# A two-layer decoder step on one core: weight folding under the recurrence, wide unit tiles in the MLP, one block stored split

## The chip, the cores and the metric

The kernel runs on one core of a Trainium2 chip. The metric is device time in microseconds: the median of three runs before is 2588.51 us (2587.13 to 2591.58). PE is TensorE, DVE is VectorE, ACT is ScalarE, POOL is GpSimd, and SP is SyncE, whose queue issues the DMAs.

## The reference, cut to what matters

1024 prompt tokens and 8 decode tokens go through two layers. Layer A is a gated linear recurrence of six heads beside a cross-attention; layer B is a sliding-window attention over keys and values made from layer A's output, again beside a cross-attention. Each layer has this frame:

```python
hn = rms_norm(h, norm_pre_mix[l])           # layer B: kv = rms_norm(h, kv_norm) @ w_kv as well
proj = hn @ w_in                            # queries, gates, values ...
mix = concat([tok_out, x_out]) @ w_out[l]
h = h + rms_norm(mix, norm_post_mix[l])
u = square(relu(rms_norm(h, norm_pre_mlp[l]) @ w_up[l]))     # 1024 -> 4096
h = h + rms_norm(u @ w_down[l], norm_post_mlp[l])            # 4096 -> 1024
```

## The kernel before, in words

Features lie on the partitions, the N = 1032 tokens on the free axis. An fp32 product is three float32r matmuls of high and low parts (`mm3`, lines 264 to 266), so each operand has to be split: ScalarE copies the high part (line 208), VectorE or GpSimd subtracts it for the low part (`tt`, line 81). `X` holds the split operand that moves through TensorE.

Outside the MLP a weight tile is 128 x 1024. It is loaded into a raw tile (tag `wr`, two buffers), split into a tile with tag `ws` (three buffers), and used for three chunks of 344 tokens (`dense_chunk`), whose sums go to a PSUM bank with tag `dn` (two of them; `ax` has four, `ac` two).

In layer A, `weave` runs the recurrence of one head (`hgrn_head`) beside the dense products of the next head. `out_late` ends the output projection. `post_norm` puts the steps of a norm on a list `bg`, from which `tick` takes them between products.

`fold_w` prepares 20 weight tiles of layer B: it loads one, multiplies 12 of them by a norm's gain on GpSimd, splits it on ScalarE and VectorE and stores both parts to DRAM (`wfd`), from which layer B loads them. Before the change these 20 calls are handed to layer A's `mlp` and run beside its down products, at the units listed in `SIDE`.

`mlp` splits both dimensions in halves and makes seven block products where eight would be plain. Up: four plain tiles, then 14 pairs of tiles with seven products each; the squared results and their sums go to DRAM as blocks "11", "12", "21", "22" and 1 to 4 (`hidden_sums`, `store`). Down: products 1, 7, 5, 6, 3, then 2 and 4, each a list of 16 units (g, m): four 128-row blocks of hidden features by one output tile. For products 1 to 3 a unit covers both chunks of 258 tokens (24 matmuls a chunk pair and g); for 2 and 4 there are separate units for each chunk. `hidden` loads a hidden block, 258 tokens at a time, into a `ct` tile and splits it into `X`; `weight_split` splits the unit's 128 x 512 weights, four units ahead. Norms of the second token half run beside product 2, that of the first half's first chunk beside product 4, the last one after it; layer B's first products (`w0`, two query tiles `cq`, the values in `swa_values`) begin beside that last one.

The code is written in program order, and a scheduler sets the order on each engine from it. In layer A the down stage takes 995.5 to 1416.6 us of the span, in layer B 2223 to 2574.4 us, with the same matmuls.

## Time and profile before

| | us |
|---|---|
| median of 3 runs | 2588.51 |
| profiled execution | 2591.9 |
| its span | 2590.1 |
| layer A: recurrence with the dense products of the next heads (part) | 190 to 560 |
| layer A: output projection and plain up tiles | 560 to 694 |
| layer A: pairs of up tiles | 694 to 995 |
| layer A: down products 1, 7, 5, 6, 3 / product 2 / product 4 | 995.5 to 1277 / to 1350.5 / to 1416.6 |
| layer B: first products | 1416.6 to 1505 |
| layer B: down products 1, 7, 5, 6, 3 / product 2 / product 4 | 2223 to 2464.4 / to 2518 / to 2574.4 |

A stage's row gives the busy time of each engine in it. PEclk is the granted TensorE clock as a share of full speed, a mean of its two levels, 1.2 and 2.4 GHz (0.5 and 1). What a wait or an edit costs is read in its own stage. The two down stages hold the same matmuls, one with folding beside it and one without.

### The profile page before, as it was taken

How to read it: one execution, taken by the hardware profiler on the slowest of the kernel's cores; microseconds unless marked ns; L12 is line 12 of the kernel's file. 1: busy time of each engine (PE TensorE's matmuls, PEld its weight loads, DVE VectorE, ACT ScalarE, POOL GpSimd, SP SyncE). 2: the span in 40 equal slices, each digit the busy share in tenths (PEclk: the TensorE clock that was granted, in tenths of full speed). 3: DMA queues.
4: the chain of work that ended last, by engine and by line, in shares of the span. 5: the costliest groups of instructions: out<-in, count | busy, mean ns of one | idle time of the engine just before them, and what ended most of it. 6: DMA issues, size and time to landing. Idle time of an engine off the chain costs nothing. (4 is left out here: it accounts for less than half of the span.)

```text
span 2590.1 us, 47277 instructions
## 1 busy us (share of the span) xinstructions
PE 2364.5 (91%) x17067; PEld 2282.3 (88%) x17067; DVE 1838.9 (71%) x3200; ACT 1159.1 (45%) x2688; POOL 1362.1 (53%) x1109
## 2 busy tenths in 40 slices
PE   7989999998889999988988799978988999999997
PEld 6889999997889998988978688768988999999996
DVE  7668666746977667898586266774587767787587
ACT  6663433534423333445554255564442333444453
POOL 4545444445755555677555243443576555446655
PEclk9999999998899999989988899989999999999998
DMA  4313222223355448777553133324336444764462
GB/s 163 132 54 100 86 83 75 74 90 115 102 176 149 144 140 273 238 254 274 181 178 109 60 111 107 117 85 150 110 105 173 152 148 136 230 184 136 111 204 85
DMA packets 265446, 362.01 MB, mean 140 GB/s; under 512 B 32938, under 2 KB 200426, under 8 KB 265196
## 3 DMA queue, kind: packets, MB, share of 16 engines
q1 hardware_dynamic: 265212, 358.99, 44.3%
q8 instruction: 134, 2.20, 0.4%
q14 instruction: 100, 0.82, 0.1%
HBM read 242.70 MB, written 112.99 MB: 137 GB/s over the span
## 5 line engine op out<-in xcount | busy, mean ns | idle before, releaser
L264 PE MATMUL dn<-X,ws 128*128 128x344 f32 (+1 forms) x1288 | 426.9, 332 | 31.2 <-DVE X L213 17.4
L265 PE MATMUL dn<-X,ws 128*128 128x344 f32 (+1 forms) x1288 | 420.2, 326 | 0.0
L266 PE MATMUL dn<-X,ws 128*128 128x344 f32 (+1 forms) x1288 | 419.8, 326 | 0.0
L81 DVE TENSOR_TENSOR X<-ct,X 128x258 fp32r<-128x258 f32 (+2 forms) x457 | 313.5, 725 | 92.6 <-ACT X L208 86.3
L81 POOL TENSOR_TENSOR ws<-wr,ws 128x512 fp32r<-128x512 f32 (+1 forms) x118 | 215.1, 1825 | 202.9 <-ACT ws L208 200.3
L264 PEld LDWEIGHTS dn<-X,ws 128*128 128x128 f32 x1288 | 250.1, 194 | 42.8 <-DVE X L213 19.8
L208 ACT CAST X<-ct 128x258 fp32r<-128x258 f32 (+2 forms) x466 | 174.7, 409 | 181.3 <-DMA ct<-u 140.2
L265 PEld LDWEIGHTS dn<-X,ws 128*128 128x128 f32 x1288 | 249.8, 194 | 1.8 <-issue 0.4
L266 PEld LDWEIGHTS dn<-X,ws 128*128 128x128 f32 x1288 | 249.4, 194 | 1.6 <-issue 0.8
L264 PE MATMUL ax<-X 128*128 128x258 f32 x736 | 208.9, 284 | 9.5 <-DVE k L81 9.5
L265 PE MATMUL ax<-X 128*128 128x258 f32 x736 | 208.8, 284 | 0.0
L266 PE MATMUL ax<-X 128*128 128x258 f32 x736 | 208.5, 283 | 0.0
L81 POOL TENSOR_TENSOR p<-p,sm 128x512 f32<-128x512 f32 (+2 forms) x92 | 83.0, 927 | 144.2 <-DVE sm L390 53.4
L208 ACT CAST ws<-wr 128x512 fp32r<-128x512 f32 (+1 forms) x122 | 95.8, 789 | 130.9 <-PE ax L266 45.9
L265 PE MATMUL ac<-X 128*128 128x258 f32 x512 | 149.4, 292 | 0.7 <-POOL X L81 0.7
L264 PEld LDWEIGHTS ax<-X 128*128 128x128 f32 x736 | 140.0, 190 | 10.6 <-DVE k L81 10.6
L266 PE MATMUL ac<-X 128*128 128x258 f32 x512 | 148.7, 290 | 0.0
L264 PE MATMUL ac<-X 128*128 128x258 f32 x512 | 148.2, 290 | 0.0
L265 PEld LDWEIGHTS ax<-X 128*128 128x128 f32 x736 | 139.9, 190 | 0.0
L266 PEld LDWEIGHTS ax<-X 128*128 128x128 f32 x736 | 139.6, 190 | 0.0
L264 PE MATMUL dn<-X 128*128 128x258 f32 x320 | 96.2, 301 | 33.1 <-DVE X L81 29.2
L81 POOL TENSOR_TENSOR X<-p,X 128x512 fp32r<-128x512 f32 (+1 forms) x56 | 82.6, 1487 | 55.1 <-ACT X L208 47.3
(645 smaller groups left out, 8128.3 us busy)
## 6 DMA issues: line engine op xcount, KB each, us to landing
ct<-u SPq DMA_DIRECT2D x480, 129.0 KB, 2.9
u<-k SPq DMA_DIRECT2D x392, 129.0 KB, 2.4
wr<-wu SPq DMA_DIRECT2D x112, 256.0 KB, 3.2
wfd<-ws SPq DMA_DIRECT2D x40, 512.0 KB, 4.1
ws<-wfd SPq DMA_DIRECT2D x26, 512.0 KB, 5.6
wr<-wia SPq DMA_DIRECT2D x25, 512.0 KB, 3.5
p<-hs SPq DMA_DIRECT2D x22, 516.0 KB, 5.3
c<-wd SPq DMA_DIRECT2D x40, 256.0 KB, 4.8
```

Of the source, the lines that this page charges most:

```text
L81: return eng.tensor_tensor(out, a, b, op=op)
L208: A.copy(hi, src)
L264: T.matmul(ps, wh, xl, start=first, stop=False, skip_group_check=more)
L265: T.matmul(ps, wl, xh, start=False, stop=False, skip_group_check=more)
L266: T.matmul(ps, wh, xh, start=False, stop=last, skip_group_check=more)
```

## The change

- The 20 calls of `fold_w` move from layer A's down stage to its recurrence, four to each of the first five heads, and each becomes two steps, load and fold. The raw weight now uses a `wr` tile, the split one a `ws` tile, and one DMA stores both parts.
- In the down stage, products 1, 7, 5, 6 and 3 load and split hidden blocks 516 tokens wide, from six places (`ust`) in two `ws` tiles.
- Block "21" is split where it is made (`split_21`, in the up pairs) and kept in DRAM as high and low parts (`u21`); product 2 loads both straight into `X`. Product 2 becomes one list of 16 units with both chunks (256 and 260 tokens; two tiles' first chunks share a bank), so its weights are split once, not twice.
- Of the weight splits' subtractions, product 2's all go to GpSimd, and of product 4's one in three to VectorE; before, every second one of both.
- `plain_sums` is cut into loads and sums, taken one at a time from the fifth pair on instead of at the second and third.
- `dense_bank`: in the output projection of layer A, in the plain up tiles of both layers and in layer B's first products, sums alternate between `ax` and `dn`.
- The norms of the down stage use `ac` banks, at a rate of 1.6 steps a unit in product 2; the last one sums eight squared rows on TensorE (`direct`) instead of adding them by fours first.
- Layer B's first products: both `cq` tiles of the token chunk that is ready come ahead of what waits for the last norm.

On ScalarE in the recurrence of layer A, between steps of a head. `ws` is a split weight, `wr` its raw tile, `k`, `q`, `t` and `r` tiles of a head. Before:

```order
L594 ACT_TABLE_LOAD
L594 ACTIVATE k_2180<-k_2179 128x344
L595 ACTIVATE k_2179<-k_2179 128x344
L208 CAST r_2272<-p_2175 128x512
L208 CAST ws_2673<-wr_2671 128x1024
```

Now:

```order
L208 CAST ws_2211<-wr_2209 128x1024
L665 ACTIVATE ct_1993<-q_1860 128x344
L705 COPY t_1677<-k_154 128x16x16 x2
L665 ACTIVATE ct_2060<-q_2029 128x344
L705 COPY t_1677<-k_154 128x8x32 x2
L208 CAST ws_2339<-wr_2242 128x1024
L705 COPY t_1677<-k_154 128x4x64 x2
L665 ACTIVATE ct_2104<-q_2029 128x344
L705 COPY t_2204<-k_1681 128x128x2 x2
L208 CAST ws_2375<-wr_2373 128x1024
```

Before, the weight cast ahead of `ws_2673` stands 16 rows further up. Now three casts of weights stand within ten rows: `ws_2211` and `ws_2375` are dense weights, `ws_2339` (raw tile `wr_2242`) is a folded one between them.

On TensorE at the end of layer A's MLP, where `t` and `p` hold the squares of the last norm and `dn_14692` is a product of layer B. Before:

```order
L265 MATMUL dn_14692<-X,p_14687 128x344
L266 MATMUL dn_14692<-X,p_14686 128x344
L160 MATMUL ax_14727<-ones,t_9943 86x1 x3
L180 MATMUL ax_14737<-ct_14735,ones 128x258
L160 MATMUL ax_14946<-ones,p_14722 86x1
L160 MATMUL ax_14946<-ones,p_14724 86x1
```

Now:

```order
L271 MATMUL ax_14428<-ws_14236,X 128x256
L272 MATMUL ax_14428<-ws_14236,X 128x256
L160 MATMUL ac_14283<-ones,t_10242 86x1 x3
L270 MATMUL dn_14300<-X,p_14294 128x344
L270 MATMUL dn_14387<-ws_14233,X 128x256
L271 MATMUL dn_14387<-ws_14233,X 128x256
```

Before, the last norm's two sums (`ax_14727`, then `ax_14946`, over squares of its input and of its output) have only the broadcast `ax_14737` between them, and the values (`dn_14781`) come after. Now the values `ax_14428` stand ahead of the first sum and a `cq` and a values product (`dn_14300`, `dn_14387`) behind it, before the broadcast.

On SP's queue in product 2 of layer A. `X` is the split operand, `u21s` the block stored split, `hs` the layer's output, `wd` weights. Before:

```order
L1307 DMA ct_13343<-u_0_5913 128x258
L1307 DMA ct_13368<-u_0_5913 128x258
L1307 DMA ct_13393<-u_0_5913 128x258
L878 DMA hs_82<-q_9918 128x258
L878 DMA hs_82<-k_9919 128x258
L878 DMA hs_82<-q_9920 128x258
L1307 DMA ct_13418<-u_0_5913 128x258
L878 DMA hs_82<-k_9922 128x258
L878 DMA hs_82<-k_9923 128x258
```

Now:

```order
L1343 DMA X<-u21s_6052 128x2x516 x8
L1296 DMA r_10234<-wd 128x512 x2
L1296 DMA r_10235<-wd 128x512
L1343 DMA X<-u21s_6052 128x2x516
L892 DMA hs_82<-q_10215 128x258
L1343 DMA X<-u21s_6052 128x2x516
L892 DMA hs_82<-k_10216 128x258
L892 DMA hs_82<-q_10217 128x258
L892 DMA hs_82<-k_10219 128x258
```

The loads of 258 tokens into `ct` became loads of both parts into `X`; eight of them, two groups of units, stand ahead of the next weights.

The diff, cut to its core:

```diff
-    def rstd_tok(*accs, square=None):
+    def rstd_tok(*accs, square=None, bank="ax"):
...
-        ps = psum("ax")
+        ps = psum(bank)
...
     def fold_w(i):
         src, base, nk = FOLDED[i]
-        raw = wpool.tile([P, 2, D], F32, tag="ws", name=nm("ws"), bufs=3)[:, 0]
-        w = wpool.tile([P, 2, D], F32R, tag="ws", name=nm("ws"), bufs=3)
...
+        def load():
+            raw = box["raw"] = wpool.tile([P, D], F32, tag="wr", name=nm("wr"), bufs=2)
+            S.dma_start(raw, src)
+
+        def fold():
+            raw = box["raw"]
+            w = wpool.tile([P, 2, D], F32R, tag="ws", name=nm("ws"), bufs=3)
+            if base is not None:
+                r = raw.rearrange("p (k f) -> p k f", k=nk)
+                tt(G, r, r, gn[:, base:base + nk].unsqueeze(2).to_broadcast([P, nk, D // nk]), ALU.mult)
+            split(raw, w[:, 0], w[:, 1], V)
+            S.dma_start(wfd[i].rearrange("h p f -> p h f"), f32(w))
+        return [load, fold]
...
+    wide, turn_ = [False], [0]
+
+    def dense_bank():
+        turn_[0] += wide[0]
+        return psum("ax" if turn_[0] % 2 else "dn")
...
-    def post_norm(Y, a, w, acc, gpost, hsrc, hdst, nxt, scaled, bank="ac"):
+    def post_norm(Y, a, w, acc, gpost, hsrc, hdst, nxt, scaled, bank="ac", rbank="ax", direct=False):
...
-            if k % 4:
+            if k % 4 and not direct:
...
-            st = rstd_tok(row(0), row(4))
+            st = rstd_tok(*(row(k) for k in range(0, KT, 1 if direct else 4)), bank=rbank)
...
+        def split_21(j, c, p):
+            hi, lo = (slot("ct", (P, CH), F32R)[:, :CW] for _ in range(2))
+            split(p, hi, lo, G)
+            for i, t in enumerate((hi, lo)):
+                S.dma_start(u21[i, j][:, c * CW:(c + 1) * CW], f32(t))
...
-                store(1, 0, c, c21[c])
+                split_21(2 + i, c, c21[c])
...
-                if i in (1, 2):
-                    for c in two:
-                        plain_sums(i - 1, c)
+                if 4 <= i and late:
+                    late.pop(0)()
...
-        units = [(p, (0, 1), u) for p in (1, 7, 5, 6, 3) for u in pairs_]
-        half = len(units)
-        units += [(p, (c,), u) for p in (2, 4) for c in range(2) for u in pairs_]
+        units = [(p, (0, 1), u) for p in (1, 7, 5, 6, 3, 2) for u in pairs_]
+        half = units.index((2, (0, 1), (0, 0)))
+        units += [(4, (c,), u) for c in range(2) for u in pairs_]
...
-            split(w, r[:, 0], r[:, 1], G if n < half or n % 2 else V)
+            split(w, r[:, 0], r[:, 1], V if p == 4 and n % 3 == 0 else G)
...
-            for c in cc:
+            if p == 2:
+                S.dma_start(f32(X[:, k, :, 0:HN]), u21[:, 4 * g + j].rearrange("h p n -> p h n"))
+                return
+            a, e = cc[0] * CW, cc[-1] * CW + CW
+            if p == 4:
                 t = chunk_tile(CW)
...
+                t = ust[nu[0] % len(ust)]
...
+            S.dma_start(t, ub[SRC[p]][4 * g + j][:, a:e])
+            split(t, X[:, k, 0, a:e], X[:, k, 1, a:e], V)
...
-            post_norm(Y, a, CW, accs[:, a:a + CW], G_POSTMLP + 8 * l, hsrc, hdst, nxt, True, "ax")
+            post_norm(Y, a, CW, accs[:, a:a + CW], G_POSTMLP + 8 * l, hsrc, hdst, nxt, True, "ac", "ac",
+                      direct=(hf, c) == (0, 1))
...
-            if side and n in SIDE:
-                side.pop(0)()
-            tick(1)
+            elif p in (2, 4):
+                tick(1.6 if p == 2 else 1)
...
-              (hgrn_sample(h, smp, osb), 0.0, 0.8), ms[4 * h - 4:4 * h] if h else [])
+              (hgrn_sample(h, smp, osb), 0.0, 0.8), ms[4 * h - 4:4 * h] if h else [],
+              [f for i in range(4 * h, 4 * h + 4) for f in fold_w(i)])
...
+    def cq_chunk(p, c):
+        if len(cq) == p:
+            cq.append(cq_pair(load_folded((1, 5)[p], ("p", "p")), p, cqs, rn))
+        dense_chunk(cq[p][1], c, cq[p][2])
+
     for n, c in enumerate((2, 1, 0)):
+        if n == 1:
+            cq_chunk(1, 2)
+        dense_chunk(w0, c, ev0)
+        if n == 0:
+            tick(1)
+            V.tensor_copy(rn, R2[:, NP_:])
+            cq_chunk(0, c)
+            tick(3)
         if n == 1:
             tick(len(bg))
...
-        dense_chunk(w0, c, ev0)
-        tick()
...
+        if n:
+            for p in range(2):
+                cq_chunk(p, c)
         swa_values(wv, vt, kvn, c, r1)
```

## Rows read from the trace of the kernel before

**Rows 1.** The page, busy time of each engine over the span: us, share, instructions.

```profile
PE 2364.5 (91%) x17067; PEld 2282.3 (88%) x17067; DVE 1838.9 (71%) x3200; ACT 1159.1 (45%) x2688; POOL 1362.1 (53%) x1109
```

**Rows 2.** Stages, from the span's start to its end: busy time of each engine.

```profile
core 0: us, PE busy (x) PEld busy (x) DVE busy (x) ACT busy (x) POOL busy (x), PEclk, DMA share, GB/s
190.00:560.00 370.00, 361.87 (x2436) 345.43 (x2436) 255.37 (x487) 152.14 (x356) 172.36 (x140) 0.99 0.28 89
560.00:694.00 134.00, 116.70 (x695) 113.22 (x693) 85.47 (x119) 57.40 (x124) 73.21 (x61) 0.90 0.26 87
694.00:755.00 61.00, 48.30 (x341) 47.09 (x342) 50.12 (x67) 19.61 (x40) 43.16 (x33) 0.87 0.58 176
995.50:1277.00 281.50, 250.63 (x1943) 246.19 (x1944) 229.83 (x292) 130.53 (x292) 185.61 (x127) 0.94 0.77 252
1277.00:1350.50 73.50, 60.01 (x431) 57.36 (x430) 59.37 (x107) 41.57 (x105) 40.59 (x39) 0.88 0.56 177
1350.50:1416.60 66.10, 56.81 (x409) 55.19 (x407) 51.80 (x80) 34.63 (x87) 39.47 (x35) 0.87 0.30 85
1416.60:1505.00 88.40, 67.07 (x466) 65.08 (x464) 26.77 (x54) 18.84 (x48) 19.94 (x21) 0.88 0.26 86
2223.00:2464.40 241.40, 236.22 (x1945) 235.01 (x1946) 178.02 (x271) 112.13 (x270) 140.49 (x115) 0.99 0.54 157
2464.40:2518.00 53.60, 49.91 (x400) 48.97 (x399) 46.10 (x83) 29.46 (x68) 30.09 (x28) 0.97 0.67 196
2518.00:2574.40 56.40, 51.19 (x396) 49.80 (x394) 45.56 (x70) 30.27 (x71) 36.00 (x30) 0.94 0.40 121
```

**Rows 3.** Who TensorE waited for, 995.5 to 1277 us: us, times, longest.

```profile
PE dn L264 <- DVE X L81: 27.3, 15, 6.0
```

**Rows 4.** Groups by line, 995.5 to 1277 us: count, busy us, mean ns, idle before.

```profile
L81 DVE TENSOR_TENSOR X<-ct,X 128x258 fp32r<-128x258 f32 x150 | 109.8, 775 | 29.3 <-ACT X L208 29.1
L81 DVE TENSOR_TENSOR ws<-ws,ws 128x1024 fp32r<-128x1024 f32 x20 | 32.5, 1626 | 7.1 <-ACT ws L208 5.6 <-DMA ct<-u 1.5
L81 POOL TENSOR_TENSOR ws<-ws,gn 128x1024 f32<-128x1024 f32 x11 | 23.3, 2114 | 19.1 <-DMA ws<-wib 8.2 <-DVE k L81 5.4 <-DMA ws<-wkv 3.7
L208 ACT CAST ws<-ws 128x1024 fp32r<-128x1024 f32 x20 | 21.0, 1049 | 31.0 <-DMA ct<-u 11.9 <-POOL ws L81 8.5 <-DMA ws<-wo 7.6
```

**Rows 5.** The same view, 2223 to 2464.4 us.

```profile
L81 DVE TENSOR_TENSOR X<-ct,X 128x258 fp32r<-128x258 f32 x150 | 96.6, 685 | 29.8 <-ACT X L208 29.5
```

**Rows 6.** The page's DMA issues: count, KB each, median us to landing.

```profile
wfd<-ws SPq DMA_DIRECT2D x40, 512.0 KB, 4.1
```

**Rows 7.** TensorE's waits, 190 to 560 us.

```profile
PE ax L718 <- DVE q L81: 6.8, 3, 3.1
```

**Rows 8.** TensorE's waits, 560 to 694 us.

```profile
PE dn L264 <- DVE k L81: 9.4, 2, 5.5
...
PE dn L264 <- ACT ct L1034: 1.8, 1, 1.8
PE dn L264 <- ACT k L948: 1.2, 1, 1.2
```

**Rows 9.** TensorE's waits, 694 to 755 us.

```profile
PE ax L264 <- DVE k L81: 6.5, 3, 3.2
```

**Rows 10.** VectorE's timeline, 1373.6 to 1442 us: start, us, instruction.

```profile
1400.91 1.75 DVE L81 TENSOR_TENSOR wr<-r,wr 128x512 fp32r<-128x512 f32 x1
...
1405.28 0.68 DVE L81 TENSOR_TENSOR ws<-wr,ws 128x512 fp32r<-128x512 f32 x1
```

**Rows 11.** Groups by line, 1277 to 1350.5 us.

```profile
L81 POOL TENSOR_TENSOR ws<-r,ws 128x512 fp32r<-128x512 f32 x2 | 2.9, 1439 | 2.0 <-ACT ws L208 2.0
...
L81 DVE TENSOR_TENSOR X<-ct,X 128x258 fp32r<-128x258 f32 x33 | 20.3, 645 | 9.2 <-ACT X L208 9.2
```

**Rows 12.** TensorE's timeline, 1424 to 1447 us.

```profile
1438.75 1.89 PE L160 MATMUL ax<-ones,p 128*86 128x1 f32 x12 [10.56 <-issue]
1445.98 0.62 PE L264 MATMUL dn<-X,p 128*128 128x344 f32 x1 [5.34 <-DMA p<-wfd]
```

98 lines of the change are left out of this document (55 added, 43 removed).

## The prediction

> **What bounds the kernel now.** I read the page first, then the stages, then in each stage who TensorE waited for. TensorE is busy 91% of the span and no other engine over 71% [rows 1], so what counts is where TensorE idles or runs at its lower clock. The stages show that this is uneven [rows 2]. The recurrence is nearly full (361.9 of 370 us). The two down stages are the clearest comparison, since their matmuls are the same. For products 1, 7, 5, 6 and 3 layer A takes 281.5 us and layer B 241.4; layer A's has 30.9 us of idle time against 5.2, and its mean granted clock is 0.94 against 0.99. Product 2 takes 73.5 against 53.6, product 4 66.1 against 56.4. After that, layer B's first products keep TensorE busy 67.1 of 88.4 us at a mean clock of 0.88. All of TensorE's 27.3 us behind split operands in layer A's long stretch end on VectorE's `X` [rows 3]: VectorE is late with the low parts, because folding is queued between them.
>
> **The change, part by part.** The terms are against the profiled execution's 2591.9 us (span 2590.1 and 1.8 around it), which is 3.4 above the median of 2588.5; the time is given on the median's scale.
>
> *Folding leaves layer A's down stage.* It takes with it 20 VectorE subtractions (32.5 us), 12 gain products on GpSimd (11 of them in this stretch, 23.3 us) and 20 ScalarE copies (21.0 us) [rows 4], and 40 stores and 20 loads. Without it the stretch should look like layer B's: 241.4 us. In both, 150 subtractions of 258 elements (mean 685 ns without folding [rows 5]) and as many copies become 75 of 516; layer B's 5.2 us of idle time is all that this can win, and I take 3. So layer A goes from 281.5 to 238.4 (-43, between -36 and -46) and layer B from 241.4 to 238.4 (-3).
>
> *Folding enters the recurrence.* The same work meets a VectorE that is busy 255 of 370 us and a GpSimd busy 172 [rows 2]; with it they stand at about 288 and 197. What hides it is that TensorE has dense products to run there. What is exposed is the head's chain, where each level goes through TensorE, VectorE, GpSimd and ScalarE: TensorE's waits for it are 6.8 us in 3 places [rows 7], and a fold puts a VectorE instruction of 1.6 us into it. And a `ws` tile is now held by a fold between two dense weights, and the dense weight's load stands in SP's queue behind the fold's store, and its cast in ScalarE's behind the fold's cast. If everything is hidden the cost is 0. The nearest row for the other end is what the same folds cost where they were, 281.5 less 241.4, or 40 us. There they stood against splits that TensorE needs within a few units; a dense weight lasts three chunks, and one fold in three tiles leaves a next weight ready. I take +10, nearer to the low end for that reason.
>
> *Product 2.* Its 32 units with 32 loads and splits of 258 become 16 units without hidden splits. From VectorE's 59.4 us in layer A go 33 splits at 645 ns and 16 weight subtractions; GpSimd keeps 16 weight subtractions at 1.44 us [rows 11] and the norms, so its 40.6 us stay. A chunk is 16 units of 12 matmuls; at layer B's 236.2 us for 1945 [rows 2] these 192 need 23.3 us, and two chunks 46.6. So GpSimd would be at 87%. Against it stands the traffic: the block comes as two parts, 16 tiles of 128 x 2 x 516 in fp32, 8.45 MB for 4.2. Layer B moves 196 GB/s in 53.6 us, 10.5 MB, at a DMA share of 0.67 [rows 2]; with 4.2 more, at 293 GB/s for a full share, this is 50 us (layer A's long stretch has 252 at 0.77, which makes 327 and 45 us). Layer A's 73.5 us at 177 GB/s hold 13.0 MB, of which early loads of layer B can move; with 4.2 more it would be 59, or 53 at 327. I take 52 for layer A (-21.5, from 46.6 to 59) and 49.5 for layer B (-4). The Trainium skill, "DMA: Bandwidth & Descriptors", Specifications, gives 358 GB/s as the limit of one core's HBM traffic; by that the two would need 48 and 41 us, and the traffic would bound only layer A. The shares in rows 2 give the lower ceilings, and I go by those.
>
> *Product 4 and layer B's first products* (154.5 us in all, 1350.5 to 1505). Product 4's first chunk is near its 23 us already. The second is bound by VectorE, which does hidden splits, every second weight split and the norm of the first chunk, and it leaves TensorE idle 9.3 us. Then the last norm's chain runs from 1416.6 to its output's sum at 1438.75, and TensorE stands 10.6 us before that sum and 5.3 us for a `cq` weight that needs the norm's `p` tiles [rows 12]. The chain stays; what changes is that one `w0` chunk, a `cq` chunk and four values products (20 us of TensorE work) may fill product 4's gaps and the chain. The idle time of the two stages is 9.3 and 21.3 us, and mean clocks of 0.87 and 0.88 mean about 38 us at 1.2 GHz, of which idle time is a part; so 40 us is the most there is. The wait for the second `cq` weight can stay (5 us). I take -22, from -8 (the chain gets longer as VectorE is no less loaded) to -32. For the splits that move to GpSimd I count nothing: the same 128x512 subtraction took VectorE 0.68 and 1.75 us within 5 us [rows 10]. Some 5 of product 4's 32 go; at the mean of the two that spares VectorE 6 us, but if the other 1.44 us [rows 11] of each on GpSimd doubles what VectorE does meanwhile, 4 of these come back. The Trainium skill, "GPSIMD Engine Reference", 1. Specifications, has a rule that speaks against this part: GpSimd shares its SBUF interfaces with VectorE and contends with VectorE instructions that have two SBUF inputs. By it the 6 us shrink to 2; where GpSimd was free of such a tie the term would be -28.
>
> *Wide banks.* With two `dn` banks TensorE waited 9.4, 1.8 and 1.2 us for their evacuation in layer A's output projection and plain tiles [rows 8]; with six banks in turn these 12.4 us should go, but the norms' chain behind them (the X waits after it) is bound by VectorE and gets only earlier by what its inputs do. I take -7, from 0 to -16. Layer B's plain tiles have one such wait: -1.5.
>
> *Pairs.* `plain_sums` leaves the second and third pair, where TensorE waited 6.5 us on VectorE sums [rows 9]: -2 in each layer. `split_21` adds 28 ScalarE copies, 28 GpSimd subtractions and 28 stores a layer, over 240 us in which TensorE is full and GpSimd half idle: 0, with 3 us as the bad end.
>
> *Product 4 of layer B and the tail.* -2 and 0: the last norm has no next norm, so `direct` changes nothing.
>
> *Sum.* Layer A: -43 + 10 - 21.5 - 22 - 7 - 2 = -85.5. Layer B: -3 - 4 - 2 - 1.5 - 2 = -12.5. Together -98: 2591.9 becomes 2493.9 profiled, and 2490.5 on the median's scale.
>
> **The rivals.**
> - *The recurrence pays in full.* The folds cost there what they cost before, 40 us instead of 10: 2520. For it: the head's chain is as dependent as the splits were. Against it: 8 us of idle time in 370 now.
> - *The ends of the down stage give nothing.* GpSimd and the DMA queues become the bound of product 2 and VectorE stays that of product 4, so 43.5 us of layer A's two terms shrink to 8, and layer B's 6 to 0: 2490 + 41 = 2531. The Trainium skill's rule on shared SBUF interfaces (same page and section) names the same mechanism.
> - *More is won.* Product 2 at its 46.6 us in both layers (-8.3 more), -32 for the ends (-10), -16 from the banks (-9): 2463.
> - *Slower.* The weight tiles become the bound of the recurrence. A fold holds its `ws` tile for its gain product, copy, subtraction and store: 2.1 + 1.05 + 1.6 + 4.1 us [rows 4, 6], 8.9 us. If TensorE stood still for all of it, 20 times, that is 178 us: 2490 - 10 + 178 = 2658. It decides from 5.4 us of standstill a fold (98 + 10 over 20). Against it: three tiles, of which a dense product uses one at a time.
> - *It does not do what it says.* The scheduler places the folds late, in the output projection, or the new order has its own waits, and gain and loss cancel: within 5 us of 2588.
>
> **How the numbers follow.** My forecast, 2470 to 2512, has 0.60; the full recurrence 0.14, the ends giving nothing 0.11, more won 0.08, slower 0.04, no effect 0.03. The likeliest time is 2490. A range from 2455 to 2535 takes in the second, third and fourth case and leaves out the last two and some of the tails. About 0.2% is what a measurement of this kernel can tell from no change: faster 0.94, within it 0.02, slower 0.04.
>
> **What would show it.** In the changed kernel layer A's products 1 to 3 should last about 240 us with hardly any wait on `X`; product 2 about 50 with no subtraction of 258-wide hidden blocks in it; the stretch from the end of product 4 to the second norm's sum should hold dense work instead of 10.6 us of standstill; the recurrence should stay above 95% busy on TensorE. I am wrong if the recurrence grows by over 25 us, or if product 2 waits for its own loads.

## The result and the profile after

The changed kernel takes 2561.02 us (median of 4 runs, 2559.91 to 2565.36), the kernel before 2589.97 beside it: a ratio of 0.9893, 95% interval 0.9875 to 0.991. It is faster by 1.1%, as forecast in sign, but by 29 us and not by 98: 2561 lies outside the range of 2455 to 2535.

First the page of the changed kernel: the busy times (answering to [rows 1]) and three of its DMA issues, with KB each and us to landing.

```profile
PE 2359.9 (92%) x17103; PEld 2276.1 (89%) x17103; DVE 1719.4 (67%) x2931; ACT 1114.9 (43%) x2493; POOL 1396.0 (54%) x1180
...
wfd<-ws SPq DMA_DIRECT2D x20, 1024.0 KB, 5.1
u21s<-ct SPq DMA_DIRECT2D x128, 129.0 KB, 3.2
X<-u21s SPq DMA_DIRECT2D x32, 516.0 KB, 6.3
```

VectorE has lost 119 us of work. TensorE has lost 5, and its idle time went from 225.6 to 203.7 us, so 22 of the 26.5 us by which the span is shorter are idle time. Where the rest of the forecast went is seen by stages. The stages of the changed kernel are cut where TensorE has streamed as many columns (summed over the matmul records of the trace) as the kernel before had at the bounds of [rows 2]; both streamed 4.55 million in all. A bound that falls into idle time of TensorE is taken at the end of that idle time, so that 694, 995.5, 1505 and 1830 us stand for 698, 996.1, 1506.2 and 1831.7; where such a pause lies at a bound, a length can be off by 1 to 3 us against its neighbour. The windows of the changed kernel, with the same columns as in [rows 2] (length, busy time and count of PE, PEld, DVE, ACT, POOL, granted clock, DMA share, GB/s):

```profile
195.20:586.20 391.00, 369.23 (x2434) 349.12 (x2433) 289.12 (x503) 164.59 (x372) 193.91 (x151) 0.97 0.47 154
...
769.90:1024.50 254.60, 242.59 (x1988) 240.11 (x1987) 165.57 (x313) 82.69 (x181) 145.51 (x133) 0.99 0.60 178
1024.50:1271.00 246.50, 238.67 (x1944) 237.15 (x1943) 157.04 (x194) 104.86 (x201) 155.93 (x122) 0.98 0.57 179
1271.00:1325.60 54.60, 51.63 (x423) 51.07 (x422) 36.07 (x62) 22.05 (x57) 35.72 (x37) 0.97 0.69 231
...
1388.00:1463.60 75.60, 72.72 (x481) 70.30 (x480) 21.39 (x46) 18.88 (x50) 18.52 (x19) 0.86 0.31 108
...
1947.80:2193.20 245.40, 231.52 (x1861) 228.99 (x1860) 156.73 (x299) 77.03 (x169) 134.52 (x124) 0.97 0.59 171
2193.20:2447.70 254.50, 239.75 (x1944) 238.05 (x1943) 165.02 (x194) 104.31 (x201) 150.56 (x122) 0.97 0.54 166
2447.70:2495.00 47.30, 47.30 (x400) 47.18 (x399) 20.55 (x42) 12.21 (x25) 26.76 (x27) 1.00 0.83 277
```

The long stretches of the pairs stand out. In the kernel before they were 240.5 and 223 us long, with TensorE full:

```profile
755.00:995.50 240.50, 239.05 (x1987) 238.85 (x1986) 167.39 (x309) 76.96 (x162) 124.05 (x102) 1.00 0.51 154
2000.00:2223.00 223.00, 222.71 (x1859) 222.50 (x1857) 157.42 (x294) 72.87 (x154) 116.58 (x96) 1.00 0.50 153
```

Now they are 254.6 and 245.4 us long, with 12 and 14 us of idle time. In layer B the same columns also kept TensorE busy 8.8 us longer (231.5 against 222.7), at a granted clock of 0.97 against 1.00. All lengths beside the forecast, in us:

| Stage (bounds of the kernel before) | before | after | change | forecast |
|---|---|---|---|---|
| start to the recurrence's end (0 to 560) | 560.0 | 586.2 | +26.2 | +10 |
| A: output projection, plain tiles, first pairs (to 755) | 195.1 | 183.7 | -11.4 | -9 |
| A: pairs, long stretch (to 995.5) | 241.0 | 254.7 | +13.7 | 0 |
| A: products 1, 7, 5, 6, 3 (to 1277) | 280.9 | 246.4 | -34.5 | -43 |
| A: product 2 (to 1350.5) | 73.5 | 54.4 | -19.1 | -21.5 |
| A: product 4 and layer B's first products (to 1505) | 155.7 | 138.2 | -17.5 | -22 |
| B: middle (to 1830) | 325.5 | 319.4 | -6.1 | 0 |
| B: output projection, plain tiles, first pairs (to 2000) | 168.4 | 164.8 | -3.6 | -3.5 |
| B: pairs, long stretch (to 2223) | 223.3 | 245.4 | +22.1 | 0 |
| B: products 1, 7, 5, 6, 3 (to 2464.4) | 241.0 | 254.6 | +13.6 | -3 |
| B: product 2 (to 2518) | 53.7 | 47.4 | -6.3 | -4 |
| B: product 4 (to 2574) | 56.0 | 52.2 | -3.8 | -2 |

The column of changes adds up to -26.7, against -26.5 between the two spans. Three things cost more than forecast: the pairs 36 us, the recurrence 16, layer B's long stretch of the down stage 17. In the pairs TensorE now waits for VectorE's evacuations, where it had waited for nothing. The waits of TensorE in layer A's long stretch of the pairs, and then in layer B's (who waits, for whom: us in total, times, longest):

```profile
PE ax L270 <- DVE k L81: 7.8, 7, 1.9
PE dn L270 <- DVE k L81: 4.2, 4, 1.3
```

```profile
PE ax L270 <- DVE k L81: 9.5, 8, 3.4
PE dn L270 <- DVE k L81: 4.4, 3, 1.8
```

Two more of TensorE's waits in the changed kernel: behind `X` in layer A's long stretch of the down stage (1024.5 to 1271 us, against [rows 3]), and the longest from 586.2 to 721.3 us, in the output projection and the plain tiles (against [rows 8]):

```profile
PE dn L270 <- DVE X L81: 2.7, 3, 1.1
```

```profile
PE dn L270 <- DVE k L81: 7.3, 3, 4.6
```

### The profile page after: what moved, and what is told of

It is laid out like the page before. It is cut to its first block, busy times and chain, and to the rows that moved or that the text cites. A ratio compares the mean times of both kernels' runs of the same rounds, so it can differ in the third digit from the quotient of the medians.

```text
span 2563.6 us, 46356 instructions
## 1 busy us (share of the span) xinstructions
PE 2359.9 (92%) x17103; PEld 2276.1 (89%) x17103; DVE 1719.4 (67%) x2931; ACT 1114.9 (43%) x2493; POOL 1396.0 (54%) x1180
## 4 chain that ended last, share of the span: by engine, by line
PE 30%; DVE 15%; DMA 10%; issue 6%; POOL 5%; ACT 3%; SPq 2%; DVEq 0%; POOLq 0%; ACTq 0%
DVE k L81 5%; PE ax L270 4%; PE ax L271 4%; PE dn L270 4%; PE ax L272 4%; PE dn L271 4%; PE dn L272 4%; DMA wr<-wu 3%; DVE X L81 2%; POOL ws L81 2%; PE ac L270 1%; PE ac L272 1%; PE ac L271 1%; POOL X L81 1%; DMA r<-r 1%
## 5 line engine op out<-in xcount | busy, mean ns | idle before, releaser
L270 PE MATMUL dn<-X,ws 128*128 128x344 f32 (+2 forms) x1176 | 395.0, 336 | 40.1 <-DVE X L213 17.8
L271 PE MATMUL dn<-X,ws 128*128 128x344 f32 (+2 forms) x1176 | 388.6, 330 | 1.7 <-POOL ws L81 1.7
L272 PE MATMUL dn<-X,ws 128*128 128x344 f32 (+2 forms) x1176 | 387.4, 329 | 0.0
L270 PEld LDWEIGHTS dn<-X,ws 128*128 128x128 f32 x1176 | 231.5, 197 | 52.4 <-DVE X L213 20.3
L271 PEld LDWEIGHTS dn<-X,ws 128*128 128x128 f32 x1176 | 232.6, 198 | 4.8 <-POOL ws L81 2.2
L272 PEld LDWEIGHTS dn<-X,ws 128*128 128x128 f32 x1176 | 232.5, 198 | 1.8 <-issue 0.8
L81 DVE TENSOR_TENSOR X<-ws,X 128x516 fp32r<-128x516 f32 x160 | 161.1, 1052 | 78.1 <-ACT X L208 77.8
L208 ACT CAST ws<-wr 128x1024 fp32r<-128x1024 f32 (+1 forms) x138 | 114.7, 832 | 149.6 <-PE ax L272 42.0
L271 PE MATMUL ac<-X 128*128 128x258 f32 x512 | 147.6, 288 | 5.8 <-POOL X L81 5.7
L272 PE MATMUL ac<-X 128*128 128x258 f32 x512 | 147.0, 287 | 0.0
L270 PE MATMUL ac<-X 128*128 128x258 f32 x512 | 146.5, 287 | 0.3 <-ACT X L208 0.3
L208 ACT CAST X<-ws 128x516 fp32r<-128x516 f32 (+1 forms) x192 | 109.7, 621 | 84.3 <-PE ax L272 49.3
L270 PE MATMUL ax<-X,ws 128*128 128x258 f32 (+2 forms) x352 | 110.6, 316 | 13.5 <-DVE k L81 13.5
## 6 DMA issues: line engine op xcount, KB each, us to landing
ws<-u SPq DMA_DIRECT2D x160, 258.0 KB, 3.6
```

The source lines that it names most:

```text
L81: return eng.tensor_tensor(out, a, b, op=op)
L208: A.copy(hi, src)
L270: T.matmul(ps, wh, xl, start=first, stop=False, skip_group_check=more)
L271: T.matmul(ps, wl, xh, start=False, stop=False, skip_group_check=more)
L272: T.matmul(ps, wh, xh, start=False, stop=last, skip_group_check=more)
```

## The experiments

Eighteen kernels were run. Stage lengths are those of the profiled execution, cut as above; "ratio" is time over the kernel before in the same job, with its 95% interval. One execution of each kernel was profiled, and it can lie several us off the median (e2_fold_alone's took 2569.7 us, m5c_pinned's 2585.3). The 13 kernels with the whole change, which do not differ up to the recurrence's end, have 580.4 to 586.2 us there. So a difference of a few us between two stage lengths is not to be read as an effect.

| Run | median us | ratio | to 560 | A pairs | A long down | B pairs | B long down |
|---|---|---|---|---|---|---|---|
| before | 2590 to 2595 | 1 | 560.0 | 241.0 | 280.9 | 223.3 | 241.0 |
| changed | 2561.0 | 0.9893 (0.9875 to 0.991) | 586.2 | 254.7 | 246.4 | 245.4 | 254.6 |
| e1_plain21 | 2552.6 | 0.9869 (0.983 to 0.9908) | 584.4 | 239.1 | 254.3 | 223.1 | 253.4 |
| e2_fold_alone | 2575.8 | 0.994 (0.9921 to 0.996) | 580.0 | 241.5 | 242.6 | 223.7 | 241.7 |
| e3_early_sums | 2554.3 | 0.9864 (0.9824 to 0.9904) | 583.2 | 258.5 | 245.8 | 237.0 | 244.9 |
| e4_sub_on_vector | 2565.4 | 0.9904 (0.9869 to 0.9938) | 583.8 | 256.6 | 254.6 | 242.4 | 258.1 |
| m1_act_queue | 2550.0 | 0.9827 (0.9791 to 0.9863) | 580.8 | 250.5 | 245.5 | 236.8 | 256.2 |
| m2_extra_store | 2558.1 | 0.9858 (0.9818 to 0.9898) | 584.4 | 242.8 | 256.8 | 224.2 | 245.8 |
| m3_cast_on_vector | 2564.9 | 0.9892 (0.9868 to 0.9916) | 580.4 | 258.0 | 257.2 | 243.8 | 254.6 |
| m4_split_on_vector | 2566.3 | 0.9905 (0.9875 to 0.9935) | 583.1 | 260.5 | 253.3 | 248.7 | 243.0 |
| m5c_pinned | 2593.2 | 1.0009 (0.999 to 1.0027) | 583.7 | 273.4 | 254.5 | 248.0 | 245.2 |
| g1_break_chain | 2541.7 | 0.9789 (0.9758 to 0.9819) | 582.1 | 239.9 | 244.3 | 224.6 | 244.5 |
| b1_cast_and_chain | 2558.4 | 0.9879 (0.9854 to 0.9903) | 580.5 | 255.5 | 246.6 | 245.1 | 243.9 |
| b4_pinned_and_chain | 2579.9 | 0.996 (0.994 to 0.9981) | 582.5 | 274.8 | 246.3 | 254.7 | 243.7 |
| f1_fold_gpsimd | 2568.7 | 0.9909 (0.9882 to 0.9936) | 582.2 | 240.0 | 240.7 | 222.9 | 241.0 |
| f2_late_folds | 2575.7 | 0.9931 (0.9906 to 0.9956) | 580.1 | 242.3 | 244.2 | 223.1 | 241.3 |
| f4_no_subtraction | 2563.3 | 0.9888 (0.9862 to 0.9914) | 577.3 | 239.6 | 242.1 | 223.5 | 241.1 |
| f6_load_cast_store | 2550.1 | 0.9842 (0.981 to 0.9874) | 562.0 | 240.8 | 241.4 | 223.4 | 242.0 |
| f8_no_gain | 2564.5 | 0.9902 (0.9869 to 0.9936) | 574.1 | 240.9 | 242.4 | 223.5 | 241.1 |
| q2_own_tile_and_chain | 2534.4 | 0.978 (0.9753 to 0.9807) | 582.4 | 239.0 | 246.3 | 226.5 | 246.2 |

### Is it the kept split that slows the pairs, or the moved sums?

e1_plain21:

```
-                split_21(j, c, ps[2])
...
-                split_21(2 + i, c, c21[c])
+                store(1, 0, c, c21[c])
...
-        SRC = {1: "11", 7: 3, 5: 1, 6: 2, 3: "22", 4: 4}
+        SRC = {1: "11", 7: 3, 5: 1, 6: 2, 3: "22", 2: "21", 4: 4}
...
-            if p == 2:
-                S.dma_start(f32(X[:, k, :, 0:HN]), u21[:, 4 * g + j].rearrange("h p n -> p h n"))
-                return
```

> The changed kernel, but block 21 of the hidden layer is stored plain in the pairs, as before the change, and product 2 loads it 516 wide and splits it with a cast and a VectorE subtraction like the other blocks. Theory 1 (the kept split is what slows the pairs: its casts, GpSimd subtractions and stores stand ahead of the next pair's weight blocks, so VectorE's block sums come late and TensorE waits behind them): the long stretch of the pairs goes from 254.6 to about 242 us in layer A and from 245.4 to about 225 in layer B, product 2 gives back 0 to 8 us a layer (16 subtractions of 1.05 us), and the total falls from 2561 to about 2530 to 2545. Theory 2 (the plain tiles' sums, now in the later pairs, do it): the pairs stay within 4 us of the changed kernel, the total is 2560 to 2577.

The pairs' long stretches are back at 239.1 and 223.1 us: theory 1's number held there. But without the kept split the sums moved too, as the section on the tiles shows, so this run alone does not separate the two. The total fell only to 2552.6, since time was given back elsewhere: the first pairs took 6.5 us (layer A) and 7.9 (layer B) longer than in the changed kernel, layer A's product 2 took 6.5, and layer A's long stretch of the down stage 7.9.

e3_early_sums:

```
-                if 4 <= i and late:
-                    late.pop(0)()
+                if i in (1, 2):
+                    for f in late[4 * (i - 1):4 * i]:
+                        f()
```

> The changed kernel, but with the sums of the plain tiles in the second and third pair of each layer, as before the change; the kept split stays. Theory 1 (the kept split slows the pairs): the long stretch of the pairs keeps most of its loss (above 250 us in layer A, above 238 in layer B), the first pairs lose the 12 us a layer that they had won, total 2570 to 2590. Theory 2 (the late sums slow the pairs): the long stretch goes back to about 242 and 225 us, the first pairs lose 12 us a layer, total 2545 to 2555.

Layer A's pairs stayed slow (258.5) and layer B's at 237.0, so the place of the sums in the program alone is not it; but the first pairs lost 0.2 us in layer A and 5.2 in layer B, not 12, so neither theory fits as it was put.

e4_sub_on_vector, in split_21:

```
-            split(p, hi, lo, G)
+            split(p, hi, lo, V)
```

> The changed kernel, with the subtraction of the kept split on VectorE instead of GpSimd; casts, stores and all else as they are. If GpSimd's order is the cause (its subtraction stands ahead of the weight blocks' splits, which release the buffers that the next loads need): the pairs win back most of the 36 us, total 2530 to 2545. If the stores' place in SyncE's queue (they wait 65 us for ScalarE's casts, ahead of the weight loads) or the traffic is the cause: within 6 us of 2561. If VectorE's own load counts: slower, above 2567.

256.6 and 242.4: GpSimd's order was not the cause.

### Stores, bytes, casts, queues

m1_act_queue, in split_21:

```
-                S.dma_start(u21[i, j][:, c * CW:(c + 1) * CW], f32(t))
+                A.dma_start(u21[i, j][:, c * CW:(c + 1) * CW], f32(t))
```

> The changed kernel, with the two stores of each kept split issued by ScalarE's DMA queue instead of SyncE's; casts, GpSimd subtractions, bytes and all else as they are. Theory 1 (place in the queue: the stores wait for cast and subtraction at the head of SyncE's queue, and the next weight blocks' loads stand behind them, so VectorE's block sums and with them the evacuations are late): the pairs' long stretch goes from 254.6 to about 242 us in layer A and from 245.4 to about 226 in layer B. Theory 2 (the added bytes, 154 to 178 GB/s in that stretch): within 4 us of the changed kernel. Rival (ScalarE's own waits for the subtraction now hold up the casts): slower than 254.6 and 245.4.

250.5 and 236.8: about a third of the loss went, neither theory's number.

m2_extra_store, on e1_plain21:

```
                 store(1, 0, c, c21[c])
+                S.dma_start(u21[0, 2 + i][:, c * CW:(c + 1) * CW], c21[c])
```

> The kernel of run e1_plain21 (block 21 stored plain), with each plain block stored a second time, so that the pairs issue as many stores and move as many bytes of this block as the changed kernel, but with no cast and no subtraction before them. Queue waits as the cause: the long stretch stays at e1's 239 us in layer A and 223 in layer B, within 3. Number of stores or bytes as the cause: about 254 and 245, as in the changed kernel.

242.8 and 224.2, at most 3.7 us of the 15.6 in layer A and 1.1 of the 22.3 in layer B: neither the number of stores nor their bytes is the main part.

m3_cast_on_vector, in split_21:

```
-            split(p, hi, lo, G)
+            V.tensor_copy(hi, p)
+            tt(G, lo, p, f32(hi), ALU.subtract)
```

> The changed kernel, with the high part of each kept split made by a VectorE copy, right behind VectorE's square of the block, instead of a ScalarE cast; GpSimd subtraction, stores and bytes as they are. Theory (ScalarE's cast waits 57 us in 21 places for VectorE's square, at the head of ScalarE's queue, and the weight blocks' casts, GpSimd's splits and the release of the weight buffers wait behind it): the pairs' long stretch goes from 254.7 to about 242 us in layer A and from 245.4 to about 226 in layer B, the first pairs keep their 48.7 and 61.2, total about 2525 to 2535. Rival (what counts is the stores' wait at the head of SyncE's queue, which stays): as in the run with ScalarE's DMA queue turned round, 250 and 240 or more, total 2550 to 2562. Second rival (VectorE's 12 us of copies a layer count in full): above 2565.

258.0 and 243.8. The theory fell: ScalarE no longer waited for the square, and the pairs were as slow.

m4_split_on_vector, with `tt(V, lo, ...)` beside the copy:

> The changed kernel, with both parts of the kept split on VectorE (copy, then subtraction), stores and bytes as they are. Theory (ScalarE's cast or GpSimd's subtraction, whichever is left there, waits 4 to 5 us a pair for VectorE's square at the head of its queue, and the weight blocks' casts and splits wait behind it): with neither there, the pairs' long stretch goes from 254.7 to 240 to 245 us in layer A and from 245.4 to 224 to 230 in layer B. Rival (the split's stores at the head of SyncE's queue, or its ct tiles): 250 or more and 240 or more. Second rival (VectorE's time counts: some 24 us more a layer): 255 or more.

260.5 and 248.7, although ScalarE and GpSimd now held no step of the kept split in the pairs. So it was not either engine's place in its queue.

m5c_pinned: split_21 is called in the pair's last step, and its cast is pinned in ScalarE's order behind what is traced before it:

```
+            x = A.copy(hi, p)
+            if pin:
+                tc.keep_in_program_order(x)
```

> The changed kernel, with the kept split's cast held behind the first products' copies of the next pair in ScalarE's order, when VectorE's square is long done; the subtraction stays on GpSimd. By the theory of waits at the head of the two queues: the pairs' long stretch 240 to 245 us in layer A and 224 to 230 in layer B, first pairs as in the changed kernel, total 2525 to 2540. Rival (the mere work on ScalarE and GpSimd, or the stores): 250 and 240 or more, total 2550 to 2565.

273.4 and 248.0, the slowest of all, where the theory wanted 240 to 245 and 224 to 230. It holds the split's two tiles longer than any other run, which was the hint to look at the tiles.

### The tiles

The kept split's parts, `hi` and `lo`, are `ct` tiles, of which there are six; the sums of the plain tiles take four of them at a time, and two more for the kept split of their own block. The loads of these sums in layer A, in SyncE's timeline (start us, us, engine, line, operation, out<-in, count), of the changed kernel and then of e1_plain21:

```profile
831.87 2.04 SPq L1082 DMA_DIRECT2D ct<-u  x4
877.02 3.32 SPq L1082 DMA_DIRECT2D ct<-u  x4
923.15 1.89 SPq L1082 DMA_DIRECT2D ct<-u  x4
967.66 1.90 SPq L1082 DMA_DIRECT2D ct<-u  x4
```

```profile
713.78 1.85 SPq L1082 DMA_DIRECT2D ct<-u  x4
725.29 1.71 SPq L1082 DMA_DIRECT2D ct<-u  x3
727.99 3.27 SPq L1082 DMA_DIRECT2D ct<-u  x2
...
746.82 0.88 SPq L1082 DMA_DIRECT2D ct<-u  x2
```

The source puts the sums into the later pairs in both kernels. Without the kept split the scheduler moves them forward into the first pairs; with it the sums sit in the long stretch, one set every second pair, each loaded right before its use. That free `ct` tiles are what decides this is the theory that q2 below tests. VectorE then stands at the head of its queue for them. Its waits there in the changed kernel, and its timeline around one of them (idle us before, and who ended it, in brackets):

```profile
DVE k L81 <- DMA wr<-wu: 34.8, 7, 8.0
DVE ct L81 <- DMA ct<-u: 18.6, 5, 5.7
DVE k L81 <- POOL X L81: 10.7, 2, 7.1
```

```profile
875.81 0.42 DVE L81 TENSOR_TENSOR k<-k,ax 128x258 f32<-128x258 f32 x1
881.90 0.43 DVE L81 TENSOR_TENSOR ct<-ct,ct 128x258 f32<-128x258 f32 x1 [5.66 <-DMA ct<-u]
...
887.72 0.74 DVE L81 TENSOR_TENSOR k<-k,dn 128x258 f32<-128x258 f32 x2
892.08 0.69 DVE L81 TENSOR_TENSOR k<-wr,wr 128x512 f32<-128x512 f32 x1 [3.61 <-POOL X L81]
```

The block sums of the next pair (`k<-wr,wr`) and the evacuations (`k<-k,dn`) come behind that wait. From one pair's first block sum to the next's it is 20.1 us in the kernel before (mean of 8 between 770 and 985 us), 22.2 in the changed kernel (mean of 8 between 785 and 1015).

Taken one by one, these distances say which pairs pay. In layer A of the changed kernel the last three before the sums' first loads are 20.1, 19.9 and 19.4 us, although each of these pairs holds the kept split in `ct`; from there on they are 21.5 to 23.3. In e3_early_sums the sums' loads stand at 767 to 810 us, later than in the kernel before and in e1, though the program has them in the second and third pair. The two distances around them are 30.2 and 31.6 us, and the last eight, which hold the kept split in `ct` but no sums, have a mean of 19.8 (17.0 to 21.0). So the kept split in `ct` alone does not slow a pair; a pair is slow where it meets the sums.

q2_own_tile_and_chain keeps the split whole and takes its two parts out of `ct`; it also has the repair of the down stage below:

```
+            kept = slot("mv", (P, 2, HN), F32R)
...
-                split_21(2 + i, c, c21[c])
+                split_21(2 + i, c, c21[c], kept)
```

`hi` and `lo` are then the two halves of `kept`, one tile for both chunks; only the plain tiles' own kept split stays in `ct`.

> The changed kernel, with the kept split's two parts in a tile of another pool (mv) instead of ct, and with one of product 6's two additions a tile on VectorE. Cast, subtraction, stores and bytes of the kept split stay as in the changed kernel; SyncE's order now has the loads of the plain tiles' sums in the first pairs, as in run e1_plain21. Theory (the split's tiles crowd the sums' loads out of ct, and VectorE then stands at its head for them): the pairs' long stretch 239 to 245 us in layer A and 223 to 229 in layer B with the whole kept split still there, first pairs 55 and 69, product 2 of layer A 53, total 2528 to 2540. Rival (the kept split's work itself, wherever its tiles are): 250 or more and 240 or more, total 2545 to 2560.

239.0 and 226.5, with cast, subtraction, stores and bytes of the kept split all in place. The sums' loads are in the first pairs, from 713 to 765 us (three of their rows here), and TensorE's waits in layer A's long stretch are down to 5 us from 12:

```profile
725.74 0.32 SPq L1082 DMA_DIRECT2D ct<-u  x1
727.10 0.41 SPq L1082 DMA_DIRECT2D ct<-u  x1
728.77 1.95 SPq L1082 DMA_DIRECT2D ct<-u  x2
```

```profile
PE dn L270 <- DVE k L81: 2.8, 1, 2.8
PE ax L270 <- DVE k L81: 2.2, 2, 1.8
```

So the kept split as work costs the pairs' long stretches next to nothing in layer A and 3.4 us in layer B (against e1's 239.1 and 223.1); its tiles, where the plain tiles' sums needed them, cost 36. That also fits m3, m4 and m5c, which all kept the split in `ct`, and e3, where the split and the sums still shared it. How much of the 36 is the sums' new place, beside a full TensorE, and how much the tiles' release, which delays them within that place, stays open: no run has the sums in the long stretch with the kept split out of `ct`. q2 is also the fastest kernel of the study, 2534.4 us: its interval of 0.9753 to 0.9807 lies wholly below the changed kernel's, and overlaps that of g1 (0.9758 to 0.9819), which stores the block plain. So whether keeping block "21" split pays at all is not clear.

### The down stage of layer B: one instruction of 15.7 us

TensorE's waits in the changed kernel's long stretch of layer B's down stage:

```profile
PE ax L270 <- DVE k L81: 8.9, 3, 6.8
PE dn L270 <- DVE X L81: 3.1, 3, 1.1
PE dn L270 <- DVE k L81: 2.8, 2, 2.3
```

The 6.8 us begin at 2402 us. VectorE's instructions that write `X` between 2391.9 and 2408.7 (count; shortest, median and longest duration in ns; first and last start; form):

```profile
L81 DVE TENSOR_TENSOR X<-ws,X x3: 682/683/15673, 2391.9 to 2408.1; 128x516 fp32r<-128x516 f32 x3
```

The same three in VectorE's timeline, which puts them into one row, and then GpSimd's timeline meanwhile:

```profile
2391.95 16.89 DVE L81 TENSOR_TENSOR X<-ws,X 128x516 fp32r<-128x516 f32 x3
2408.76 0.41 DVE L81 TENSOR_TENSOR k<-k,ax 128x258 f32<-128x258 f32 x1
```

```profile
2384.09 2.65 POOL L81 TENSOR_TENSOR k<-k,ct 128x258 f32<-128x258 f32 x4
2386.68 1.32 POOL L81 TENSOR_TENSOR X<-t,X 128x512 fp32r<-128x512 f32 x1
2387.93 2.66 POOL L81 TENSOR_TENSOR k<-k,ct 128x258 f32<-128x258 f32 x4
...
2402.08 3.69 POOL L81 TENSOR_TENSOR X<-p,X 128x512 fp32r<-128x512 f32 x3
2405.74 1.32 POOL L81 TENSOR_TENSOR t<-t,ct 128x258 f32<-128x258 f32 x2
```

The first of three equal subtractions took 15.67 us, the other two 0.68 each. GpSimd ran without a gap from 2382.6 to 2407.1, and the subtraction ended 0.6 us after that. After TensorE's standstill its granted clock was lower as well, 0.74 from 2400 to 2420 us. The same instruction took 15.64 to 15.69 us at this place in seven other profiles (in e1_plain21, e4 and m3 in both layers, in m1, m2, m4 and m5c in one). In the kernel before, in e3_early_sums and in layer A of the changed kernel itself none was held, although the last two have the same instructions at this place. What decides it was not found.

g1_break_chain, on e1_plain21, in product 6's evacuation:

```
-                tt(G, c21, c21, t, ALU.add)
+                tt(V, c21, c21, t, ALU.add)
```

> The kernel of run e1_plain21, with one of product 6's two additions a tile on VectorE instead of GpSimd. Theory (one VectorE subtraction with both inputs in SBUF was held for 15.66 us while GpSimd ran 22 instructions without a gap, and TensorE stood 6.8 us for it, in both layers): no VectorE instruction above 4 us, the end of products 6 and 3 shorter by 7 to 10 us in each layer, total 2533 to 2540. Rival (VectorE was late for another reason, its trace record is wrong): TensorE stands as long as before, total 2550 to 2556.

No VectorE instruction was above 4 us, and the two long stretches went from 254.3 and 253.4 us to 244.3 and 244.5. b1_cast_and_chain and b4_pinned_and_chain set the same line beside m3 and m5c:

> The changed kernel with both repairs: the high part of the kept split made by VectorE, and one of product 6's two additions a tile on VectorE instead of GpSimd. By the theories of runs m3_cast_on_vector and g1_break_chain together: pairs as in the first, ends of products 6 and 3 shorter by 7 to 10 us in layer B and by 0 to 3 in layer A (where the changed kernel had no such stall), total 2512 to 2527. If only the chain's repair works: 2545 to 2553.

> Run m5c_pinned with one of product 6's two additions a tile moved from GpSimd to VectorE as well. If both repairs hold: another 7 to 10 us in layer B's products 6 and 3, and as much in layer A where m5c_pinned has a VectorE instruction above 15 us there, total 2510 to 2530. If they don't add up: no faster than the better of the two, 2541.

Their totals missed, because the repairs of the pairs did (255.5 and 245.1; 274.8 and 254.7). The line itself gave 8 to 11 us wherever there had been such an instruction: b1 against m3, 257.2 to 246.6 and 254.6 to 243.9; b4 against m5c in layer A, 254.5 to 246.3, and in layer B, where m5c had none, 245.2 to 243.7.

### What a fold costs the recurrence

e2_fold_alone is the kernel before with `fold_w` and its place from the changed kernel:

> The kernel before, with the folding moved to the recurrence and nothing else of the change. Theory 1 (the folds cost the recurrence about 21 us from 195 to 586 us and a few before it, and give the down stage of layer A 35 us): 2590 + 26 - 35, about 2581, recurrence about 391 us. Rival (the recurrence pays about 10, as predicted, and what else it lost comes from other parts of the change): about 2555 to 2565, recurrence about 380 us. Second rival (the folds pay nothing and the down stage gains the full 43): 2547.

580.0 us to the recurrence's end, +20.0, and the long stretch of layer A's down stage at 242.6, -38.3; nothing else moved by over 3.2 us. TensorE's waits from 192.8 us to the recurrence's end, the largest, against [rows 7]:

```profile
PE ax L724 <- DVE q L81: 5.9, 5, 1.8
PE ac L780 <- DVE r L766: 3.0, 4, 1.1
PE ax L794 <- DVE c L81: 2.8, 2, 2.3
PE ax L570 <- DVE s L574: 2.5, 1, 2.5
```

They are many short waits for the head's chain, none for a weight tile `ws`.

f2_late_folds, on e2, puts no folds beside the first two heads and 7, 7 and 6 beside the next three:

> The kernel of run e2_fold_alone, with no folds beside the first two heads and 7, 7 and 6 beside the next three, instead of 4 beside each of five. Theory 1 (the cost depends on the place: beside the second head, 190 to 250 us of the kernel before, VectorE is busy 93% already, and 12 of the 20 us were lost there): the stretch to 560 us of the kernel before's work takes 564 to 570 instead of 580, total 2560 to 2567. Theory 2 (each fold costs 1 us wherever it is): about 580, total 2572 to 2580. Theory 3 (tiles: more folds a head take the tiles that the dense weights need): above 585.

580.1. Theory 1 had started from too high a figure: in the kernel before VectorE is busy 51.6 of the 60 us from 190 to 250 (86%). The first two heads had their old time again (190.0 and 58.7 us to 190 and from there to 250), and the next three paid for it: a fold costs 1.0 us (20 us over 20) here or there.

f1_fold_gpsimd has `split(raw, w[:, 0], w[:, 1], G)` in the fold:

> The kernel of run e2_fold_alone, with the folds' subtractions on GpSimd (2.4 us each by the dense weights' rows) instead of VectorE (1.24 us). If a fold costs its VectorE time, because VectorE's chain bounds the head: work to 560 us of the kernel before takes about 562 to 568 instead of 580. If it costs what it takes of ScalarE, the weight tiles or the queues: 578 to 582. If GpSimd's time weighs as much, being in the head's chain and in VectorE's way: 585 to 600.

582.2, just above the second outcome's 578 to 582. As I read it with f6 below, what VectorE was spared, GpSimd's 2.4 us took back.

f4_no_subtraction has a second cast in place of the subtraction, f8_no_gain leaves the gain products out, and f6_load_cast_store leaves both out and stores the one cast twice:

> The kernel of run e2_fold_alone, with the folds' subtraction left out: the low part is a second ScalarE cast of the weight, so layer B's products with the low parts of its folded weights are not what the reference computes. Nothing of the folds is left on VectorE; the gain products on GpSimd, casts, loads and stores stay. If a fold costs its VectorE time: work to 560 us of the kernel before takes 560 to 566 instead of 580. If it is the rest (ScalarE casts that wait for tiles, GpSimd's gain products): 575 to 585.

> The kernel of run e2_fold_alone, with the folds' 12 gain products on GpSimd left out, so layer B's folded weights lack their gains and the outputs behind them are not the reference's. Cast, VectorE subtraction and store stay. If GpSimd's products (2.06 us each, 25 us) are the main part of the folds' cost: work to 560 us of the kernel before takes 564 to 570 instead of 580. If VectorE's subtractions (1.24 us each, 25 us) are: 575 to 580. If both together only, because either alone fills the head's chain: 572 to 578.

> The kernel of run e2_fold_alone, with the folds' gain products and subtractions left out: a fold loads its weight, casts it and stores the cast twice, so layer B's products with folded weights are not what the reference computes. If the folds cost by their time on VectorE and GpSimd: work to 560 us of the kernel before takes 560 to 564 instead of 580. If by the tiles, ScalarE's queue and the transfers: 573 to 580.

577.3, 574.1 and 562.0. Without the two steps the folds cost 2 us in all, though their loads, casts, tiles and stores are there. Without one of them they still cost 17 or 14. So it is the two steps on VectorE and GpSimd together, 18 of the 20 us. The savings of one alone, 2.7 and 5.9, come to less than the 18.0 of both, but 2.7 is within the scatter between profiles and 5.9 hardly above it. f4's second ScalarE cast may be part of why its share is small, and f6 also holds its `ws` tile for less time; neither was tried by itself.

## Why the prediction was wrong

The steps that failed are three terms of the sum: the kept split in the pairs at 0, the folds in the recurrence at +10, and layer B's down stage at -3. Step by step, in the prediction's own order:

- **Folding leaves layer A's down stage.** Right in mechanism: TensorE's 27.3 us behind `X` in [rows 3] became 2.7. Alone (e2) it gave 38.3 us, with the wider splits 34.5, against 43. The 516-wide splits, taken to win 3 us a layer, showed no gain: with no held instruction the stretch is 244 to 246 us in g1 and q2, in both layers, against 242.6 with the narrow ones in layer A (e2) and 241.0 in layer B (before). Why it is not shorter was not tried.
- **Folding enters the recurrence.** The term was +10 and measured +20 alone. The step that failed is the choice of the low end, "nearer to the low end for that reason": the reason was weight tiles, and with loads, casts, stores and tiles all in place f6 costs 2 us. The price is the work on VectorE and GpSimd, which the prediction had counted (255 to 288 and 172 to 197 us), had placed in the head's chain, and held mostly hidden by TensorE's dense work. The changed kernel's +26.2 is 6 above e2; other kernels with the whole change have 580.4 to 584.4, so part of these 6 is scatter. From 195.2 to 586.2 us TensorE was also busy 3.6 us longer than in e2 for the same columns (369.2 against 365.7), at a granted clock of 0.97 against 0.99. The rival of the full 40 us was off by 20 on the other side of e2's +20, and the slower rival's tile standstill did not appear. Of the prediction's own signs, "above 95% busy" failed (369.2 of 391.0 us, 94.4%), and "grows by over 25 us" depends on the start: +21.0 from the bound at 190 us, +26.2 from 0.
- **Product 2.** Right: -19.1 and -6.3 against -21.5 and -4, and in layer B TensorE is busy all 47.3 us at 277 GB/s and a DMA share of 0.83, so the doubled traffic did not bound it there. In neither layer did TensorE wait for the block's loads: in layer A its waits above 0.1 us are 2.1 and 0.9 us, both behind VectorE.
- **Product 4 and layer B's first products.** Right: -17.5 against -22, within -8 to -32. The standstill of 10.6 us [rows 12] is gone; from 1388 to 1463.6 us no wait on TensorE is over 1.0 us. The Trainium skill, "GPSIMD Engine Reference", 1. Specifications, says that GpSimd and VectorE share SBUF interfaces. By that rule the prediction's 6 us for the moved splits shrink to 2, which would make its term -24, and without such a tie -28; the measured -17.5 falls short of both and of the -22, so it decides nothing on the rule, and the part of the splits was not measured by itself.
- **Wide banks and the sums' move.** Together -11.4 against -9 in layer A, but the agreement is partly luck. The output projection and the plain tiles (560 to 698) went from 138.0 to 135.0, 3 us where the forecast had 7, and the first pairs (698 to 755) from 57.1 to 48.7, 8 us where it had 2. Of the 12.4 us of waits that the six banks were to remove, the 9.4 behind VectorE's `k` were still 7.3.
- **The pairs.** This is the largest error: `split_21` at "0, with 3 us as the bad end", and -2 for the sums. Measured +13.7 and +22.1 in the long stretches. "240 us in which TensorE is full and GpSimd half idle" priced the engines and left out two things: the tiles that the new step takes from a pool in use, and that the scheduler may place other work by which tiles are free. q2 shows that the engines' part was in fact about 0 in layer A and 3.4 us in layer B.
- **Layer B's down stage.** -3 forecast, +13.6 measured. Some 9 us of it go with the held VectorE instruction (e1 against g1, 253.4 to 244.5), which no row of the kernel before shows on VectorE. Without it the stretch is still 3 to 5 us longer than before (244.5 in g1, 246.2 in q2, against 241.0); that part is open.
- **Product 4 of layer B and the tail.** -3.8 against -2, and 0.
- **Layer B's middle** was not in the forecast: -6.1. It varies from 318.7 to 325.7 us over the kernels of this study, none of which changes anything there, so -6.1 is within that scatter; its cause was not looked for.

The misses add up: 35.8 (pairs), 16.6 (layer B's long stretch), 16.2 (recurrence), 8.5 (layer A's long stretch), 4.5 (product 4 and first products) and 2.4 (layer A's product 2) make 84 us; 6.1, 2.4, 2.3, 1.8 and 0.1 were won beyond the forecast elsewhere; the rest is the 71 us between 98 and 27. The chance of "faster" was right. The range failed because the tiles (36 us) and the held instruction (some 9) were not among the rivals: without the pairs' 36 us alone the time would be about 2525, inside it, and q2, which repairs both, took 2534. The forecast had also summed ten terms of which each was allowed to miss only by itself.

## What to carry to other kernels

Before a step is costed at nothing under an idle engine, ask which tiles it holds and who else draws on that pool: here a pool of six moved other work back by 118 us and more and cost 36 us, and another pool's tile made the same step nearly free. When work moves beside a chain of short dependent steps, charge a good part of its time on the chain's engines, though TensorE is busy next to it: here 18 us for some 25 us on VectorE and 23 on GpSimd. And look in the trace for single instructions many times longer than their kind, which sums and means hide.
